# RWKV blocks of a hybrid decoder layer: three bursts laid out on four quadrants, the group norm's passes moved to ScalarE, and the buffers, loads and order that go with it

## The chip, the cores and the metric

The kernel runs on one core of a Trainium2 chip. A core has a matrix engine (TensorE, PE in the rows; its weight loads are a row kind of their own, PEld) and three others that work on tiles: VectorE (DVE), ScalarE (ACT) and GpSimd (POOL). SyncE (SP) issues most DMA transfers. Each engine takes its instructions strictly in the order in which the program lists them and waits, where it must, on semaphores of the others. The metric is the device time of one execution in microseconds (us), the median of several runs.

## The reference

One decoder layer on 2048 tokens of width 1024. An adaLN-modulated RMS norm feeds one input projection. Half of its columns go to an RWKV-7 group (8 heads of 64), half to a stick-breaking attention group. Both are gated, projected out together and added back. The change lies in the RWKV group:

```python
def step(state, inp):
    r_t, w_t, k_t, v_t, kk_t, b_t = inp
    sa = jnp.einsum('bhij,bhj->bhi', state, -kk_t)
    state = (state * w_t[:, :, None, :]
             + sa[..., None] * b_t[:, :, None, :]
             + v_t[..., None] * k_t[:, :, None, :])
    y_t = jnp.einsum('bhij,bhj->bhi', state, r_t)
    return state, y_t
...
mean = jnp.mean(y, axis=-1, keepdims=True)
var = jnp.mean(jnp.square(y - mean), axis=-1, keepdims=True)
y = (y - mean) * lax.rsqrt(var + GN_EPS)
y = y * ln_w.reshape(H, N) + ln_b.reshape(H, N)
y = y + jnp.sum(rf * kf * r_k, axis=-1, keepdims=True) * vf
return y * jax.nn.silu(g)
```

The kernel doesn't step token by token. It takes chunks of 64 tokens; inside a chunk the recurrence becomes a triangular 64x64 system, which is inverted, and only one state per chunk is carried on.

## The kernel before

The first part of the program (norm, projections of the attention group, attention; up to about 1036 us) is left as it is. From about 1044 us the RWKV group runs in 16 blocks. Block n is one pair of heads (j = 0 to 3) and 512 tokens (b = 0 to 3, eight chunks); b = 0 begins a new pair. A block's work is written as stages, and the loop of step n interleaves three streams by weights: `stage_c(n)`; `stage_gtl(n)`, which runs the group norm of block n-1 (`stage_g`), then `stage_t`, `stage_l` and `stage_z` of block n+1; and `stage_pw(n+2)` with `stage_p` (projections, keys, the chunk matrices and their inversion). Each `yield` hands over to another stream, and its number is the cost that the interleaving books. A scheduler then turns the listing into one fixed order for each engine.

What each stage does, by tile names and lines:
- `stage_p`: 72 matmuls `pss` of 128x512 a block (L370 to L372) project r, k and v; ACT (L399) and DVE (L400 to L403) shift them by a token. `stage_x` makes the chunk matrices with two bursts `x` (L974), each with four masking operations on DVE (L979) that write `mn` and `mt`. Then `mn` goes out (`dn`, L986, SP) and comes back in rows as `pb` (L988). `invert` solves the 16x16 diagonal pieces on DVE (L789 to L816), writes them out (`dt`, L992) and loads them as `t16` (L997), whose second half `t16[:, 1]` is the inverse's diagonal.
- `stage_t`: transposes into `tmp`, `vp`, `ap`, then burst `bvp` (L1033); ACT copies the results (L1013, L1021, L1027, L1036).
- `stage_l`: burst `fp` (L1047) takes `mn` and `t16`; DVE masks it (`ft`, L1051); three bursts `xp` with additions (`rf`) finish the inverse.
- `stage_z`: burst `zp` (L1080), copied by ACT into `at` (L1084) and `zg` (L1088); bursts `mr` (L1096), `np` (L1110) and `y0` (L1113); DVE makes `mtt` and `rq` (L1101, L1103), `n0` (L1116).
- `stage_c`: eight chunk steps, each a matmul `sp` (L1134) and a DVE operation `sall` (L1135), then burst `yr` (L1144) and the sum `ysb` (L1148).
- `stage_g`: statistics of `ysb` on DVE (L1163, L1164), `vr` (L1166), the power -1/2 on POOL (L1167), two passes over `ysb` on POOL (L1169, L1170), the transposes `ytp` (L1174), and the additions and the gate.

`burst()` holds a list of small matmuls together as one unbroken row on TensorE. `z_ps`, `mm_ps`, `tr_ps` and `av_ps` hand out PSUM tiles; `z_ps` has two buffers, which `x`, `zp`, `np`, `y0`, `fp` and `xp` share, so a burst waits until the copies of the tile two before it are done. Matrices of 64x64 use a quarter of the array (a quadrant: 64 rows by 64 columns); `HS[e]` is one half of the partitions. In the bursts `mr` and `yr` all four quadrants are used; in `fp`, `bvp` and `zp` an operand's half and the result's half are the same or tied, so that two quadrants are.

Of the kernel before, what the change touches and what calls it, by code (L numbers as in the profile page):

```python
# [18 lines left out]
P = 128  # L19
# [69 lines left out]
def trunk(nc, a, out):  # L89
# [10 lines left out]
    words = 23848  # L100
# [40 lines left out]
    crow = cp.tile([8, P], F32, name="crow")  # L141
# [12 lines left out]
    rows = cp.tile([P, P], F32, name="rows")  # L154
# [208 lines left out]
    pace = [None]  # L363

    def inproj(w, b, name):
        wh, wl = w[0], w[1]
        ps = mm_ps(name)
        for k in range(KB):
            with tc.issue_after(pace[0]) if pace[0] is not None else nullcontext():
                PE.matmul(ps, wh[:, k], hth[b][:, k], start=k == 0, stop=False)  # L370
            PE.matmul(ps, wh[:, k], htl[b][:, k], start=False, stop=False)  # L371
            PE.matmul(ps, wl[:, k], hth[b][:, k], start=False, stop=k == KB - 1)  # L372
            yield 0.65
        return ps
# [445 lines left out]
    @contextmanager  # L820
    def burst():
# [7 lines left out]
        mms = behind + [i for i in traced[start:] if i.engine == first[0].engine]  # L829
        behind[:] = mms[-1:]  # L830
# [21 lines left out]
    def stage_p(n):  # L852
# [9 lines left out]
        else:  # L862
            lz = [rp_.tile([P, TB], F32R, tag=t, name="lz" + t) for t in ("lw", "th")]
# [94 lines left out]
    def stage_x(n):  # L958
# [43 lines left out]
    def stage_t(n):  # L1002
# [24 lines left out]
        A.activation(out=ab[:, :, :, 0, :].rearrange("p i h d -> p (i h) d"),  # L1027
                     in_=ap.rearrange("p (c d) -> p c d", c=8), func=AF.Copy)
        bvp = z_ps("bvp").rearrange("p (c d) -> p c d", c=8)
        with burst():  # L1030
            for i, h in IH:
                for e in (1, 0):
                    PE.matmul(bvp[HS[e], 2 * i + h], mn[i // 2][HS[1 - e], e, i % 2, h], zg[HS[1 - e], e, i, h],  # L1033
                              start=True, stop=True)
        yield 0.9
        A.activation(out=ab[:, :, :, 1, :].rearrange("p i h d -> p (i h) d"), in_=bvp, func=AF.Copy)  # L1036

    def stage_l(n):
# [32 lines left out]
    def stage_z(n):  # L1071
# [4 lines left out]
        zp = [z_ps("zp").rearrange("p (c m d) -> p c m d", c=4, m=2) for _ in range(2)]  # L1076
# [74 lines left out]
    def stage_g(n):  # L1151
# [28 lines left out]
    def stage_pw(n):  # L1180
# [4 lines left out]
        yield from stage_p(n)  # L1185
        if j < 3:
            if b > 0:
                yield from w_split(("rk", "rr", "rv")[b - 1], j + 1)
            if b < 3:
                w_load(("rk", "rr", "rv")[b], j + 1)  # L1190

    def stage_gtl(n):
# [6 lines left out]
        if n + 1 < NST:  # L1199
            yield from stage_l(n + 1)  # L1200
# [9 lines left out]
    _merge((stage_gtl(-1), 13.5), (stage_pw(1), 22))  # L1210
# [81 lines left out]
    for n in range(NST):  # L1292
        jobs = [(_prio(tc, stage_c(n), 100), 13), (stage_gtl(n), 17.5)]
# [42 lines left out]
```

## Time and profile before

| | |
|---|---|
| median of 3 runs | 1912.5 us (1912.26 to 1915.36) |
| the profiled execution | 1910.53 us, its span 1908.8 us |
| mean granted TensorE clock | 0.971 of full speed |
| busy: PE, DVE, ACT, POOL | 90%, 71%, 46%, 40% of the span |
| RWKV blocks, start of `fp` to start of the next | 37.1 to 46.0 us, 15 intervals from 1101.5 to 1722 us, 41.4 us on average |

The profiled execution lies 2.0 us below the median. A row of a timeline gives the start, the duration, the engine, the line and operation, the tiles (output<-inputs) with their shapes, a count of like instructions in succession, and in brackets the idle time of the engine before it and what ended that. Matmuls overlap, so the duration of a row of many is best read from the starts of the rows.

### The profile page before, as it was taken

What the parts mean: (1) busy time and instruction counts of PE and PEld (TensorE: products, weight loads), DVE (VectorE), ACT (ScalarE), POOL (GpSimd) and SP (SyncE); (2) the same over time, 40 slices, a digit from 0 to 9 for tenths busy, and PEclk for the clock granted to TensorE, in tenths of its full rate; (3) what the DMA queues carried; (4) which work ended last, traced back from release to release, by engine and by line L of the source; (5) the groups of instructions that cost most, each with busy time, mean ns of one, the idle gap of its engine ahead of it and who ended that gap; (6) DMA issues with size and microseconds to landing.
All of it is one profiled execution on the core that took longest, in us unless ns stands there. A gap on an engine that the chain in (4) does not pass through costs nothing. (4 is left out here: it accounts for less than half of the span.)

```text
span 1908.8 us, 38922 instructions
## 1 busy us (share of the span) xinstructions
PE 1719.8 (90%) x14880; PEld 1161.5 (61%) x14880; DVE 1348.7 (71%) x2855; ACT 870.0 (46%) x1718; POOL 754.6 (40%) x1106
## 2 busy tenths in 40 slices
PE   7979889999899998999997898898899888989998
PEld 2646556666566665667654455665555565667886
DVE  4876788577776778768775667877877777775542
ACT  2665567366654656546654333323332333422221
POOL 1425466355643646445444223222223232223322
PEclk9889999999999999999998899999999999999999
DMA  8442201222123221132111423222333333236442
GB/s 298 150 116 56 56 26 50 64 64 70 37 56 81 67 56 42 51 92 67 45 50 56 133 55 83 68 60 74 77 81 81 80 77 107 75 94 179 149 138 89
DMA packets 210408, 159.93 MB, mean 84 GB/s; under 512 B 113247, under 2 KB 171820, under 8 KB 210222
## 3 DMA queue, kind: packets, MB, share of 16 engines
q1 hardware_dynamic: 209220, 155.31, 29.2%
q8 instruction: 117, 1.92, 0.4%
q10 hardware_dynamic: 1002, 2.13, 0.4%
q14 instruction: 69, 0.57, 0.1%
HBM read 94.48 MB, written 44.04 MB: 73 GB/s over the span
## 5 line engine op out<-in xcount | busy, mean ns | idle before, releaser
L523 POOL TENSOR_TENSOR s<-s,u 128x512 f32<-128x512 f32 (+2 forms) x320 | 305.8, 963 | 216.5 <-ACT s L511 102.0
L540 DVE TENSOR_TENSOR al<-tr,ah 128x512 fp32r<-128x512 f32 (+1 forms) x320 | 187.4, 599 | 96.3 <-ACT ah L539 95.7
L522 DVE TENSOR_TENSOR_SCAN u<-u,dmask 128x512 f32<-128x512 f32 x192 | 240.0, 1268 | 13.0 <-ACT u L510 11.4
L539 ACT ACTIVATE ah<-tr 128x512 fp32r<-128x512 f32 (+1 forms) x320 | 171.7, 553 | 103.7 <-PE tr L535 99.6
L510 ACT ACTIVATE u<-z 128x512 f32<-128x512 f32 (+2 forms) x320 | 173.4, 555 | 73.4 <-PE z L507 49.0
L535 PE MATMUL tr<-kept_ident,s 128*128 128x128 f32 x1088 | 173.5, 279 | 33.1 <-DVE al L540 26.5
L511 ACT ACTIVATE s<-z 128x512 f32<-128x512 f32 (+2 forms) x320 | 166.2, 549 | 53.0 <-PE tr L535 53.0
L535 PEld LDWEIGHTS tr<-kept_ident,s 128*128 128x128 f32 x1088 | 130.3, 143 | 74.9 <-DVE al L540 38.4
L370 PE MATMUL pss<-kept_hh,kept_wh 128*128 128x512 f16 x416 | 161.3, 388 | 8.8 <-PEq L730 8.8
L372 PE MATMUL pss<-kept_hh,kept_wl 128*128 128x512 f16 x416 | 160.9, 387 | 0.0
L371 PE MATMUL pss<-kept_hl,kept_wh 128*128 128x512 f16 x416 | 160.9, 387 | 0.0
L372 PEld LDWEIGHTS <-kept_wl 128*128 128x128 f16 x928 | 93.2, 100 | 104.9 <-issue 14.2
L370 PEld LDWEIGHTS <-kept_wh 128*128 128x128 f16 x928 | 94.3, 102 | 101.4 <-issue 29.2
L371 PEld LDWEIGHTS <-kept_wh 128*128 128x128 f16 x928 | 93.0, 100 | 94.8 <-issue 25.0
L506 PE MATMUL z<-kt,qt 128*128 128x512 f32 (+2 forms) x320 | 132.1, 417 | 9.5 <-issue 3.7
L553 PE MATMUL av<-ah,vt 128*128 128x512 f32 (+1 forms) x320 | 136.5, 427 | 3.9 <-DVE o L564 2.3
L554 PE MATMUL av<-al,vt 128*128 128x512 f32 (+1 forms) x320 | 136.0, 426 | 0.2 <-DVE al L540 0.2
L507 PE MATMUL z<-kt,qt 128*128 128x512 f32 (+2 forms) x320 | 117.5, 371 | 0.0
L519 DVE TENSOR_TENSOR_SCAN u<-u,dmask 128x128 f32<-128x128 f32 (+3 forms) x128 | 107.3, 867 | 11.6 <-ACT u L510 6.6
L370 PE MATMUL psg<-kept_hh,kept_wh 128*128 128x512 f16 x256 | 99.1, 387 | 10.9 <-DVE klo L434 4.8
L1274 PE MATMUL po<-kept_woh,kept_yh 128*128 128x512 f32 x256 | 102.3, 400 | 0.0
L1275 PE MATMUL po<-kept_wol,kept_yh 128*128 128x512 f32 x256 | 101.5, 397 | 0.0
(296 smaller groups left out, 4146.1 us busy)
## 6 DMA issues: line engine op xcount, KB each, us to landing
kept_raw<-in_w_in SPq DMA_DIRECT2D x29, 512.0 KB, 4.3
ad<-in_ada_w SPq DMA_DIRECT2D x24, 512.0 KB, 5.6
qt<-qt SPq DMA_DIRECT2D x48, 256.0 KB, 3.3
xt<-in_x SPq DMA_DIRECT2D x16, 512.0 KB, 5.1
y<-sg SPq DMA_DIRECT2D x32, 256.0 KB, 2.3
t<-dt SPq DMA_DIRECT2D x64, 128.0 KB, 3.2
xr<-in_x SPq DMA_DIRECT2D x16, 512.0 KB, 3.6
out<-xr SPq DMA_DIRECT2D x16, 512.0 KB, 2.6
```

What stands on the lines that cost most here:

```text
L370: PE.matmul(ps, wh[:, k], hth[b][:, k], start=k == 0, stop=False)
L371: PE.matmul(ps, wh[:, k], htl[b][:, k], start=False, stop=False)
L372: PE.matmul(ps, wl[:, k], hth[b][:, k], start=False, stop=k == KB - 1)
L510: A.activation(out=u[:, 0:nk], in_=z[:, 0:nk], func=AF.Sigmoid, scale=-0.125)
L511: A.activation(out=s[:, 0:nk], in_=z[:, 0:nk], func=AF.Sigmoid, scale=0.125)
L522: V.tensor_tensor_scan(out=ur, data0=ur, data1=mr, initial=u[:, nk:nk + 1], op0=ALU.mult, op1=ALU.bypass)
L523: G.tensor_tensor(out=s[:, 0:nk], in0=s[:, 0:nk], in1=u[:, 1:nk + 1], op=ALU.mult)
L535: PE.transpose(tp[:, q * P:(q + 1) * P], att[gi, q][:, ks * P:(ks + 1) * P], ident)
L539: A.activation(out=ah[:, r], in_=tp[:, r], func=AF.Copy)
L540: V.tensor_tensor(out=al[:, r], in0=tp[:, r], in1=ah[:, r].bitcast(F32), op=ALU.subtract)
L553: PE.matmul(av[:, r], vs, ah[:, r], start=first, stop=False, skip_group_check=True)
L554: ins = PE.matmul(av[:, r], vs, al[:, r], start=False, stop=last, skip_group_check=True)
```

## The change

Three bursts are laid out anew. In `fp`, `bvp` and `zp` the half of the output is now `e ^ h` or depends on it, so that each burst goes over all four quadrants. `fp` and `bvp` each fill half of two PSUM tiles (one of `z_ps`, one of `mm_ps`), so that the operations that read them are two in place of one. Each of the two `zp` tiles is now filled by matmuls of the whole burst; `at` is copied by four operations of 64x256 in place of two of 128x256, `zg` by four of 64x256 as before. The copy of `ap` becomes four operations. `t16[:, 1]` changes its halves by parity, and its load becomes four DMAs in place of two.

The group norm's two passes on POOL go; a small DVE operation `nm` makes -mean times `vr`, and eight ACT operations of 128x64 (one per head and 128 tokens) apply `vr` as scale and `nm` as bias.

The rest: `fp`'s burst is tied behind the latest projection matmul that has been listed (`burst(True)`); five more `yield`s stand ahead of `stage_l`, and two stream weights change; `lz` (the low-rank columns) has two buffers of its own in place of those of `lw` and `th`; `invert` takes its scratch from `at`'s buffer; the load of the next pair's weights stands after the ninth `yield` of the next block's `stage_p` in place of at the end of a block; two small tiles of the first part move to another pool.

```diff
-        fp = z_ps("fp").rearrange("p (c d) -> p c d", c=8)
-        with burst():
+        fp = [f("fp").rearrange("p (i d) -> p i d", i=8) for f in (z_ps, mm_ps)]
+        with burst(True):
             for i, h in IH:
                 for e in (1, 0):
-                    PE.matmul(fp[HS[e], 2 * i + h], mn[i // 2][HS[e], e, i % 2, h], t16[HS[e], 0, 2 * i + h],
+                    PE.matmul(fp[e][HS[e ^ h], i], mn[i // 2][HS[e], e, i % 2, h], t16[HS[e], 0, 2 * i + h],
                               start=True, stop=True)
-        V.tensor_tensor(out=ft, in0=fp, in1=_bc(fmask, [P, 8, 64]), op=ALU.mult)
+        for e in range(2):
+            V.tensor_tensor(out=ft[:, e::2], in0=fp[e][:, 0:4], in1=_bc(fmask, [P, 4, 64]), op=ALU.mult)
...
-                    PE.matmul(zp[i // 2][HS[e], 2 * (i % 2) + h].rearrange("p m d -> p (m d)"), rf[HS[e], 2 * i + h],
-                              ab[HS[e], i, h].rearrange("p m d -> p (m d)"), start=True, stop=True)
-        yield 1.8
-        for g in range(2):
-            A.activation(out=at[:, 2 * g:2 * g + 2].rearrange("p i h d -> p (i h) d"), in_=zp[g][:, :, 0, :],
-                         func=AF.Copy)
+                    f = e ^ h
+                    PE.matmul(zp[f][HS[e], i].rearrange("p m d -> p (m d)"), rf[HS[f], 2 * i + e],
+                              ab[HS[f], i, e].rearrange("p m d -> p (m d)"), start=True, stop=True)
+        yield 0.9
+        for e in range(2):
+            for h in range(2):
+                A.activation(out=at[HS[e], :, h, :], in_=zp[e ^ h][HS[e], :, 0, :], func=AF.Copy)
...
-        G.tensor_tensor(out=y8, in0=y8, in1=_bc(mv[:, :, 0:1], [P, 8, 64]), op=ALU.subtract)
-        G.tensor_tensor(out=y8, in0=y8, in1=_bc(vr, [P, 8, 64]), op=ALU.mult)
+        nm = sm.tile([P, 8, 1], F32, name="nm")
+        V.scalar_tensor_tensor(out=nm, in0=mv[:, :, 0:1], scalar=-1.0, in1=vr, op0=ALU.mult, op1=ALU.mult)
+        for q in range(8):
+            yq = ysb[:, q // 2, q % 2]
+            A.activation(out=yq, in_=yq, func=AF.Identity, scale=vr[:, q], bias=nm[:, q])
...
         if n + 1 < NST:
+            for _ in range(5):
+                yield 0.6
             yield from stage_l(n + 1)
...
-    _merge((stage_gtl(-1), 13.5), (stage_pw(1), 22))
+    _merge((stage_gtl(-1), 14.5), (stage_pw(1), 22))
...
-        jobs = [(_prio(tc, stage_c(n), 100), 13), (stage_gtl(n), 17.5)]
+        jobs = [(_prio(tc, stage_c(n), 100), 13), (stage_gtl(n), 18.2)]
```

The fixed order of the engines changes with it. The block shown is the one whose `fp` starts at 1228.25 us in the profile of before. On ScalarE, around its `stage_z` (`t` is a projection of v on its way, `y` the copy of `y0`), before:

```order
L399 ACTIVATE t_20255<-pss,kept_um_19416 128x512
L331 ACTIVATE kept_wl_314<-kept_ident_61,m_20489 128x128
L1084 ACTIVATE at<-zp 128x256
L1088 ACTIVATE zg<-zp 64x256 x2
L1084 ACTIVATE at<-zp 128x256
L1088 ACTIVATE zg<-zp 64x256 x2
L1118 ACTIVATE y_20493<-y_20437 128x512
L399 ACTIVATE t_20473<-pss,kept_um_19965 128x512
```

and now, with the lines of the new program:

```order
L332 ACTIVATE kept_wl_317<-kept_ident_61,m_20702 128x128
L400 ACTIVATE t_20319<-pss,kept_um_19446 128x512
L1188 ACTIVATE ysb<-ysb,nm,vr 128x64
L1102 ACTIVATE at<-zp 64x4x64 x4
L1105 ACTIVATE zg<-zp 64x4x64 x4
L400 ACTIVATE t_20545<-pss,kept_um_20014 128x512
L1188 ACTIVATE ysb<-ysb,nm,vr 128x64 x7
L1134 ACTIVATE y_20543<-y_20460 128x512
```

One of the eight group-norm operations now stands ahead of the copies of `zp`, and the projection `t` of v directly behind them. This is the order in 11 of the 16 blocks; in three of the four with b = 0 the copies stand first, and the first block has no group norm at that place.

On VectorE, from `vr` of the group norm over the masks of the second burst `x` to the operations on `mr`, before:

```order
L1166 TENSOR_SCALAR vr<-mv 128x8
L979 TENSOR_TENSOR mn<-x_20338,kept_xmask_240 128x4x64
L979 TENSOR_TENSOR mt<-x_20338,kept_xmask_240 128x2x2x64
L979 TENSOR_TENSOR mn<-x_20339,kept_xmask_240 128x4x64
L979 TENSOR_TENSOR mt<-x_20339,kept_xmask_240 128x2x2x64
L1101 TENSOR_TENSOR mtt<-mr,kept_id_70 64x4x64 x2
```

and now:

```order
L1182 TENSOR_SCALAR vr<-mv 128x8
L1185 SCALAR_TENSOR_TENSOR nm<-mv,vr 128x8
L401 COPY t_20704<-nxt 128x1
L403 COPY nxt<-t_20545 128x1
L404 SCALAR_TENSOR_TENSOR vt<-pss,kept_u_20015,t_20545 128x512
L985 TENSOR_TENSOR mn<-x_20402,kept_xmask_243 128x4x64
L985 TENSOR_TENSOR mt<-x_20402,kept_xmask_243 128x2x2x64
L985 TENSOR_TENSOR mn<-x_20403,kept_xmask_243 128x4x64
L985 TENSOR_TENSOR mt<-x_20403,kept_xmask_243 128x2x2x64
L1117 TENSOR_TENSOR mtt<-mr,kept_id_70 64x4x64 x2
```

The operation `nm` and the one on v (`vt`, which reads ACT's `t`) have come between `vr` and the masks. This is so in six blocks.

On TensorE, from the last matmul of the first burst `x` to the start of the second, before:

```order
L974 MATMUL x_20288<-ar,bk 64x128
L1080 MATMUL zp<-ab,rf 64x128 x16
L370 LDWEIGHTS kept_wh_287
L370 MATMUL pss<-kept_hh_384,kept_wh_287 128x512
L974 MATMUL x_20338<-ar,bk 64x128
```

and now:

```order
L980 MATMUL x_20352<-ar,bk 64x128
L1097 MATMUL zp<-ab,rf 64x128
L371 LDWEIGHTS kept_wh_290
L371 MATMUL pss<-kept_hh_387,kept_wh_290 128x512
L372 LDWEIGHTS kept_wh_290
L372 MATMUL pss<-kept_hl_388,kept_wh_290 128x512
L373 LDWEIGHTS kept_wl_291
L373 MATMUL pss<-kept_hh_387,kept_wl_291 128x512
L371 LDWEIGHTS kept_wh_290
L371 MATMUL pss<-kept_hh_387,kept_wh_290 128x512
L1097 MATMUL zp<-ab,rf 64x128 x15
L372 LDWEIGHTS kept_wh_290
```

The burst `zp` is parted after its first matmul by four matmuls `pss`, and the last row shown begins eight more that stand ahead of the second `x`; before there was one. (The program lists the 16 matmuls of a burst `zp`; the trace has each twice, x32.)

## Rows read from the trace of the kernel before

**Rows 1.** Windows: stretch, its length, busy time of PE, PEld, DVE, ACT, POOL, clock.

```profile
1200.00:1300.00 100.00, 91.87 (x1261) 61.27 (x1261) 78.30 (x240) 34.63 (x63) 28.69 (x25) 1.00 0.30 71
```

**Rows 2.** Waits of TensorE, 1150 to 1690 us (13 blocks): total, times, longest.

```profile
PE sp L1134 <- DVE sall L1135: 15.7, 20, 1.7
PE zp L1080 <- DVE mt L979: 11.4, 10, 1.2
PE pn L924 <- ACT sq L916: 8.2, 8, 3.4
PE y L1113 <- DVE mt L979: 4.5, 3, 1.5
```

**Rows 3.** Timeline of TensorE in one block, and `fp` of a later one.

```profile
1228.25 1.15 PE L1047 MATMUL fp<-t,mn 64*64 64x64 f32 x32
1229.34 0.39 PE L372 MATMUL pss<-kept_hh,kept_wl 128*128 128x512 f16 x1
1229.56 0.38 PE L370 MATMUL pss<-kept_hh,kept_wh 128*128 128x512 f16 x1
...
1234.79 0.69 PE L1144 MATMUL yr<-sall,rq 64*64 64x64 f32 x32
1235.30 1.06 PE L974 MATMUL x<-ar,bk 64*64 64x128 f32 x32
1236.19 1.04 PE L1080 MATMUL zp<-ab,rf 64*64 64x128 f32 x16
1238.46 1.09 PE L1080 MATMUL zp<-ab,rf 64*64 64x128 f32 x16 [1.23 <-DVE mt L979]
...
1266.64 1.15 PE L1047 MATMUL fp<-t,mn 64*64 64x64 f32 x32
...
1353.26 1.15 PE L1047 MATMUL fp<-t,mn 64*64 64x64 f32 x32
```

**Rows 4.** Timeline of ScalarE in the same block: copies of `zp`, and `t` of v.

```profile
1239.59 0.38 ACT L1084 ACTIVATE at<-zp 128x256 f32<-128x256 f32 x1 [1.27 <-PE zp L1080]
1239.87 0.76 ACT L1088 ACTIVATE zg<-zp 64x256 f32<-64x256 f32 x2
...
1246.96 0.69 ACT L399 ACTIVATE t<-pss,kept_um 128x512 f32<-128x512 f32 x1 [2.52 <-PE pss L372]
```

**Rows 5.** Timeline of GpSimd in the same block: the group norm.

```profile
1240.66 1.64 POOL L1167 TENSOR_TENSOR vr<-vr,kept_mhalf 128x8 f32<-128x8 f32 x1
1242.38 1.04 POOL L1170 TENSOR_TENSOR ysb<-ysb,vr 128x512 f32<-128x512 f32 x1
```

**Rows 6.** Timeline of VectorE in the same block, and the inversion's last step of the later one.

```profile
1239.55 0.17 DVE L1166 TENSOR_SCALAR vr<-mv 128x8 f32<-128x8 f32 x1
...
1241.96 0.41 DVE L979 TENSOR_TENSOR mt<-x,kept_xmask 128x256 f32<-128x256 f32 x1
...
1248.02 0.17 DVE L794 COPY pr<-pb 64x8 f32<-64x8 f32 x1 [0.61 <-DMA pb<-dn]
...
1248.31 0.74 DVE L403 SCALAR_TENSOR_TENSOR vt<-pss,kept_u,t 128x512 f32<-128x512 f32 x1
...
1256.58 0.37 DVE L816 COPY pr<-pr 64x256 f32<-64x256 f32 x1
...
1341.57 0.37 DVE L816 COPY pr<-pr 64x256 f32<-64x256 f32 x1
```

**Rows 7.** Timeline of SyncE's issues in the same block, and the page's row of them.

```profile
1259.12 3.10 SPq L997 DMA_DIRECT2D t<-dt  x4
t<-dt SPq DMA_DIRECT2D x64, 128.0 KB, 3.2
```

**Rows 8.** The tile `fp`: idle time of its engine until this load, and times.

```profile
  DMA t<-dt: 2.6, 1
```

**Rows 9.** Timeline of TensorE after its longest wait.

```profile
1305.97 1.14 PE L924 MATMUL pn<-kept_hm,sq 128*128 128x2 f32 x8 [3.40 <-ACT sq L916]
1307.35 0.63 PE L370 MATMUL pss<-kept_hh,kept_wh 128*128 128x512 f16 x1
```

More of the change, by code (lines that the diff above doesn't have):

```diff
@@ L139, in trunk @@
     V.tensor_copy(out=id2[64:128], in_=ident[64:128, 64:128])
-    crow = cp.tile([8, P], F32, name="crow")
+    sbk = stage.enter_context(ExitStack())
+    kp = sbk.enter_context(tc.tile_pool(name="kv", bufs=1))
+    xctx = ExitStack()
+    rowp = xctx.enter_context(tc.tile_pool(name="rows", bufs=1))
+    crow = rowp.tile([8, P], F32, name="crow")
     DMA.dma_start(out=crow, in_=a["c"][0].rearrange("(r c) -> r c", c=P))
@@ L153, in trunk @@
     V.tensor_tensor(out=cact, in0=cact, in1=cps[:, 0:8], op=ALU.mult)
-    rows = cp.tile([P, P], F32, name="rows")
+    rows = rowp.tile([P, P], F32, name="rows")
     col = {}
@@ L371, in inproj @@
             PE.matmul(ps, wh[:, k], htl[b][:, k], start=False, stop=False)
-            PE.matmul(ps, wl[:, k], hth[b][:, k], start=False, stop=k == KB - 1)
+            latest[0] = PE.matmul(ps, wl[:, k], hth[b][:, k], start=False, stop=k == KB - 1).ins
             yield 0.65
@@ L820, in burst @@
     @contextmanager
-    def burst():
+    def burst(proj=False):
         traced = tc.nc.cur_bb.bb.instructions
@@ L829, in burst @@
         mms = behind + [i for i in traced[start:] if i.engine == first[0].engine]
+        if proj:
+            new = next(i for i in mms if i not in behind)
+            tc.add_manual_dep(new, latest[0].name, mybir.DependencyInfo(mybir.DependencyClass.NoSync,
+                                                                        mybir.DependencyReason.DATA), reason="burst")
         behind[:] = mms[-1:]
@@ L862, in stage_p @@
         else:
-            lz = [rp_.tile([P, TB], F32R, tag=t, name="lz" + t) for t in ("lw", "th")]
+            lz = [rp_.tile([P, TB], F32R, tag=f"lz{m}", name="lz") for m in range(2)]
             for m in range(2):
@@ L995, in stage_x @@
         for e in range(2):
-            for m in range(2):
-                DMA.dma_start(out=t16[HS[e], m], in_=dt[m, e].rearrange("c s t -> s c t")[0:64])
+            DMA.dma_start(out=t16[HS[e], 0], in_=dt[0, e].rearrange("c s t -> s c t")[0:64])
+        for e in range(2):
+            for f in range(2):
+                DMA.dma_start(out=t16[HS[f], 1].rearrange("p (i x) t -> p i x t", x=2)[:, :, e],
+                              in_=dt[1, e].rearrange("(i h) s t -> h s i t", h=2)[e ^ f, 0:64])
     IH = [(i, h) for i in range(4) for h in range(2)]
@@ L1026, in stage_t @@
         yield 0.44
-        A.activation(out=ab[:, :, :, 0, :].rearrange("p i h d -> p (i h) d"),
-                     in_=ap.rearrange("p (c d) -> p c d", c=8), func=AF.Copy)
-        bvp = z_ps("bvp").rearrange("p (c d) -> p c d", c=8)
+        apv = ap.rearrange("p (i h d) -> p i h d", i=4, h=2)
+        for h in range(2):
+            for e in range(2):
+                A.activation(out=ab[HS[e ^ h], :, e, 0, :], in_=apv[HS[e], :, h, :], func=AF.Copy)
+        bvp = [f("bvp").rearrange("p (i d) -> p i d", i=8) for f in (z_ps, mm_ps)]
         with burst():
@@ L1032, in stage_t @@
                 for e in (1, 0):
-                    PE.matmul(bvp[HS[e], 2 * i + h], mn[i // 2][HS[1 - e], e, i % 2, h], zg[HS[1 - e], e, i, h],
+                    PE.matmul(bvp[e][HS[e ^ h], i], mn[i // 2][HS[1 - e], e, i % 2, h], zg[HS[1 - e], e, i, h],
                               start=True, stop=True)
-        yield 0.9
-        A.activation(out=ab[:, :, :, 1, :].rearrange("p i h d -> p (i h) d"), in_=bvp, func=AF.Copy)
+        yield 0.5
+        for e in range(2):
+            A.activation(out=ab[:, :, e, 1, :], in_=bvp[e][:, 0:4], func=AF.Copy)
     def stage_l(n):
@@ L1075, in stage_z @@
         at = rw.tile([P, 4, 2, 64], F32, tag="at", name="at")
-        zp = [z_ps("zp").rearrange("p (c m d) -> p c m d", c=4, m=2) for _ in range(2)]
+        zp = [z_ps("zp").rearrange("p (i m d) -> p i m d", i=4, m=2) for _ in range(2)]
         with burst():
@@ L1184, in stage_pw @@
             rw_start(j)
[L1185 to L1190, printed above, removed]
+        for i, c in enumerate(stage_p(n)):
+            yield c
+            if i == 8 and j < 3 and b > 0:
+                w_load(("rk", "rr", "rv")[b - 1], j + 1)
+        if j < 3 and b > 0:
+            yield from w_split(("rk", "rr", "rv")[b - 1], j + 1)
     def stage_gtl(n):
```

22 lines of the change are left out of this document (10 added, 12 removed).

## The prediction, as it was put on record

> **What bounds the kernel now.** I read the windows first. In the RWKV stretch TensorE is busy 92% of the time and VectorE 78%, while ScalarE and GpSimd stand near a third [rows 1]; the clock is at its full 2.4 GHz level there. TensorE is therefore the first account: what it is spared counts unless it turns into a wait. The waits of TensorE come next. The four largest groups of 13 blocks, 15.7, 11.4, 8.2 and 4.5 us [rows 2], are 39.8 us, or 3.1 us a block; most blocks could not gain more by removing waits alone. The timeline of one block comes third: `fp` starts at 1228.25 and at 1266.64 us, a period of 38.4 us, and TensorE's row is nearly closed [rows 3].
>
> A second account runs beside it, since the rows of a block depend on each other from one to the next. I follow it in the same block, from the start of `zp` at 1236.19 [rows 3]. The second burst `x` gives the masks, and the last one ends at 1241.96 + 0.41 = 1242.37, 6.2 us after the start. Through two DMA steps (out to `dn` and back as `pb`) the inversion starts at 1248.02, 5.65 us later, and its last copy at 1256.58, after 8.56 us [rows 6]. The four loads of `t16` are issued from 1259.12 over 3.1 us, and one lands 3.2 us after its issue [rows 7]: the last issue is near 1261.5, the landing near 1264.7, 8.1 us after the copy. `fp` starts 1.9 us behind that [rows 3], and 7.94 us lie between `fp` and its `zp` (1228.25 to 1236.19). 6.2 + 5.65 + 8.56 + 8.1 + 1.9 + 7.94 is again 38.4. So this loop over `zp`, masks, inversion, `fp` has a reserve of only 1.9 us; in the later block of the rows the copy is at 1341.57 and `fp` at 1353.26, 11.7 us, a reserve of 3.6 [rows 3, 6]. In one block it was used up: `fp` waited 2.6 us for the load [rows 8].
>
> **The change part by part.** *Bursts.* `fp` takes 1.09 us from its start to the next row's; `yr`, as many matmuls of the same shape in four quadrants, takes 0.51 (1234.79 to 1235.30). That spares 0.58, and as much for `bvp`, which has the same shape and count. `zp` takes two halves of 1.04 and 1.09 by their durations, 2.04 by the pitch of about 1.02 each; `x`, as many matmuls of its shape in four quadrants, takes 0.89 (1235.30 to 1236.19) [rows 3]. That spares 1.1. Together 2.26 us a block, or 36 us in 16. All of it is TensorE time in a stretch where TensorE is busy, so all of it counts in the first account.
>
> *Copies.* A copy of 256 columns takes 0.38 us on ScalarE for 128 partitions and 0.76 / 2 for 64 [rows 4]: halving the partitions saves nothing. `at` and `zg` go from six copies (2.3 us) to eight (3.0 us). The halves of the `ap` copy go from one operation to four of the 256-column kind, 4 x 0.38 = 1.5 us. With ScalarE busy a third, this time itself is covered; what counts is who waits for the last copy. Before, the copies of the first half ran while the second half was still waiting; now every `zp` tile needs the whole burst, and so all copies come after it.
> The Trainium skill says in "TensorEngine Tiling (Array Packing)", Performance Considerations, PSUM Bottleneck, that tiling makes TensorE faster but not the evacuation of PSUM, which may then be the limit. The trace agrees, with a burst of 0.9 us and copies of 3.0. By this rule alone `zp`'s share, 1.1 x 16 = 18 of the 36 us, would be lost; the forecast below takes the loss from the order of the copies instead.
>
> *Group norm.* Two passes of 1.04 us each (one stands in the rows) leave GpSimd [rows 5], which TensorE did not wait for. Eight operations of 128x64 go to ScalarE: between 0.2 and 0.38 us each (no row shows the shape; the 256-column copies bound it above, and below I halve them), 0.3 taken, 2.4 us a block. The cost is in the order. In 11 blocks the first of the eight stands ahead of `at`. It needs `nm`, that needs the power on GpSimd, and that needs `vr`, which starts only at 1239.55, 3.36 us after `zp` [rows 6]. From `zp`'s start: `vr` done at 3.5, power 1.64 [rows 5] to 5.2, `nm` 0.17 to 5.4, one operation to 5.7. Only then can `at` be copied, at 3.4 us before (1239.59 [rows 4]). Four copies end at 7.2, three of `zg` at 8.35. The second `x` needs the PSUM tile that this seventh copy frees. TensorE reaches it with a first `zp` matmul, the wait for the masks of the first `x` until 2.27 (1238.46 [rows 3]; the four `pss` between lie inside it), the other 15 until 3.2 and eight `pss` at 0.22 (1229.34 to 1229.56 [rows 3]) at 4.9. The **new wait is 3.4 us**, in 11 blocks 37 us: what the bursts spared. Only waits further on in a block (`sp`, `pn`, `y`) could shrink for it.
>
> *The loop.* In six of those blocks the masks of the second `x` also stand behind `vt`, which needs ScalarE's `t` of v behind the eight copies: copies to 8.7, `t` 0.69 [rows 4] to 9.4, `vt` 0.74 [rows 6] to 10.2, four masks at 0.35 to 11.6. That is 5.4 later than 6.2. In the other five the masks follow `x` (8.35 + 0.9) at 10.7, 4.5 later. The rest of the loop is as it was: 5.65 + 8.56 + 8.1, and 7.94 less 0.58. The loads of `t16` are six, but the pair that `fp` needs is still within the first six issues of SyncE, where the old four and the two `dt` were; I take no difference, and 0.8 us (one issue of 3.1 / 4 [rows 7]) as an end. So the block of the rows goes from 38.4 to 11.6 + 5.65 + 8.56 + 8.1 + 7.36 = 41.3, **2.9 us longer**. Its TensorE account would give 38.4 - 2.26 + 3.4 = 39.5; the longer one decides.
>
> *Sum.* Six blocks at 2.9 are 17. Two blocks, the second and third of the first pair, have `mr` ahead of the second `x`, waiting for `at`; I take 3 each, 6. Three blocks have the masks at 10.7 and longer periods before; between 1.1 (TensorE account) and 2.0 (loop), 1.5 each, 4.5. In three blocks with b = 0 the copies stand first: the bursts' 2.26 less one for the eight copies, -1 each, -3. The first block and the last one's tail have no such wait, -2 each, -4. Together +20.5 on 1910.5, and 2.0 for the distance to the median: **1933 us**.
>
> *The rest.* Own buffers for `lz` let it load earlier (nobody waits for it in the rows): nothing, and 1 us gain at most. The five `yields` and the pin of `fp` move `pss` ahead of `fp`; if `fp` is late anyhow, this costs nothing. The weight load moves out of the way of `dt` on SyncE: 0 to 0.8 us gain in nine blocks. The two halves of `ft` (2 x 0.41 in place of 0.69, from the masks' duration) cost 0.1 a block.
>
> **The rivals.** *Faster, the wait is absorbed (24 in 100).* If the inversion and the loads shorten or the reserve is nearer to 3.6 than 1.9 in most blocks, the loop stays covered; the new wait of 3.4 then takes the place of the waits for `sall`, `sq` and `y`'s masks, 15.7 + 8.2 + 4.5 = 28.4 in 13 blocks, 2.2 a block [rows 2]. A block then gains 2.26 + 2.2 - 3.4 = 1.06, 17 us: 1895. Everything spared and no wait at all would be 1912.5 - 36 = 1876. It decides whether `t16` lands before TensorE arrives at `fp`. Against it: 1.9 us of reserve where 5.4 is asked for.
>
> *No change that can be told (8 in 100).* TensorE's account alone balances: 37 us of waits against 36, with a part absorbed: 1909 to 1916. (A measurement of this kernel tells 0.2%, 3.8 us, from none.)
>
> *Slower still, by the clock (8 in 100).* After the longest wait of TensorE, 3.40 us, six `pss` in a row took 0.63 us in place of 0.38 (the first stands in the rows [rows 3, 9]): the lower level of 1.2 GHz. If each of 11 waits of that length brings six at 0.25 more, 1.5 us, this adds 16.5: 1950. For it: the length is the same. Against: one such spell is all I see, and near it TensorE had shorter waits as well.
>
> *The bursts don't shorten (2 in 100)*, because halves of one tile hinder each other: 1933 + 36 at most where TensorE decides, about 1955 with the loop deciding in half of the blocks. `yr` and `x` speak against it.
>
> **How the numbers follow.** The forecast, slower through the loop, has 58 in 100, with a range of its own of 1916 to 1949: the reserve at 3.6 in place of 1.9 in all 11 blocks takes 17 off, the 0.8 at the loads and longer group-norm operations (0.08 x 8) in 11 blocks add 16. With the faster case included and the two slowest cases cut at the edge, the range is 1890 to 1952. Chances: faster 0.24, same 0.08, slower 0.68.
>
> **What would show it.** Right, if the profile of the changed kernel has TensorE waiting some 3 us at the second `x` in most blocks, put down to ScalarE's `zg`; if `fp` waits for the load of `t16` in six blocks or more, and the plain block's period is 41 us. The bursts are right if `fp` takes 0.5 and `zp` 0.9 from start to start; the wait's cause, if the first 128x64 operation ends 5.7 us after `zp`. Wrong, if `vr` comes much earlier than 3.4 us after `zp`, if `fp` starts without a wait, or if the waits at `sp` go.

## The result, and the profile after

| | before | after |
|---|---|---|
| median of 4 runs each | 1912.38 us (1912.15 to 1915.36) | 1966.54 us (1965.37 to 1968.87) |
| profiled execution, its span | 1910.53, 1908.8 us | 1965.89, 1964.0 us |
| mean granted TensorE clock | 0.971 | 0.953 |

The change makes the kernel slower: the medians lie 54 us apart, and the ratio on record is 1.0265, with an interval of 1.0240 to 1.0291 (46 to 56 us). The direction was forecast, the size was not: +20.5 was expected, and the time lies beyond the range.

The windows come first. The columns are stretch, length, busy time of PE, PEld, DVE, ACT and POOL (with counts), granted clock, share and rate of the DMAs. The RWKV part from 1040 us to the end, of before:

```profile
1040.00:1908.80 868.80, 780.87 (x8954) 536.05 (x8954) 581.16 (x1647) 270.54 (x499) 249.08 (x228) 0.98 0.35 95
```

and of after:

```profile
1040.00:1964.00 924.00, 791.21 (x8954) 533.01 (x8954) 586.63 (x1681) 337.90 (x723) 213.24 (x196) 0.93 0.33 89
```

TensorE executes the same 8954 matmuls. It is idle for 132.8 us in place of 87.9, and it is busy for 10 us more although three bursts became shorter. The clock, 0.93 in place of 0.98, is why. To part the two, I took all TensorE rows of this stretch, from the start of each to the start of the next. The first row is the first projection of the RWKV part, at 1044.89 us before and 1046.45 after. Idle time (from 0.15 us on) is "waits"; half of the busy time at the granted clock of 0.5 (the 1.2 GHz level) is "clock"; the rest is "work", as it would be at 2.4 GHz. The half is an estimate: the slow `mr` shown below loses 0.77 of its 1.75 us.

| RWKV part to the end | waits | clock | work |
|---|---|---|---|
| before | 71.8 | 15.5 | 767.2 |
| after | 116.0 | 49.3 | 742.7 |
| difference | +44.2 | +33.8 | -24.5 |

The sum, +53.5, is the longer stretch but for 1.7 us, and 1.6 of these lie ahead of the first row. So the bursts did spare TensorE some 25 us, new waits took 44, and the slower clock took 34 beside them. The 1.2 GHz level held for 34 us in 7 stretches before, for 118 us in 22 stretches after (those that begin behind the first row).

The waits of TensorE after (1150 to 1690 us, total, times, longest), the counterpart of [rows 2]:

```profile
PE x L980 <- ACT zg L1105: 22.5, 7, 3.9
PE sp L1150 <- DVE sall L1151: 15.0, 14, 1.6
PE pn L930 <- ACT sq L922: 12.1, 11, 2.5
PE fp L1062 <- DMA t<-dt: 10.3, 5, 3.6
PE zp L1097 <- DVE mt L985: 8.3, 9, 0.9
PE mr L1112 <- ACT at L1102: 5.8, 2, 3.4
```

The first, fourth and last line are new. `sp` is hardly smaller than in [rows 2], `zp` is smaller by a quarter, and `pn` is larger by half. A plain block on TensorE, as [rows 3] shows it of before:

```profile
1240.47 0.81 PE L1062 MATMUL fp<-t,mn 64*64 64x64 f32 x32 [1.71 <-DMA t<-dt]
1241.21 0.65 PE L944 MATMUL n<-kept_ident,nr 128*128 128x128 f32 x4
...
1247.45 1.05 PE L980 MATMUL x<-ar,bk 64*64 64x128 f32 x32
1248.34 0.38 PE L1097 MATMUL zp<-ab,rf 64*64 64x128 f32 x2
1248.65 0.39 PE L371 MATMUL pss<-kept_hh,kept_wh 128*128 128x512 f16 x1
...
1250.60 1.10 PE L1097 MATMUL zp<-ab,rf 64*64 64x128 f32 x30 [0.92 <-DVE mt L985]
1251.63 0.39 PE L372 MATMUL pss<-kept_hl,kept_wh 128*128 128x512 f16 x1
...
1253.15 0.38 PE L373 MATMUL pss<-kept_hh,kept_wl 128*128 128x512 f16 x1
1256.55 1.10 PE L980 MATMUL x<-ar,bk 64*64 64x128 f32 x32 [3.02 <-ACT zg L1105]
1257.48 1.05 PE L1112 MATMUL mr<-mt,at 64*64 64x128 f32 x32
1258.46 1.15 PE L1126 MATMUL np<-zg,mt 128*64 128x64 f32 x32
```

Its releasers on GpSimd, ScalarE and VectorE (compare [rows 4 to 6]):

```profile
1251.95 1.64 POOL L1183 TENSOR_TENSOR vr<-vr,kept_mhalf 128x8 f32<-128x8 f32 x1 [7.17 <-DVE vr L1182]
```

```profile
1253.82 0.44 ACT L1188 ACTIVATE ysb<-ysb,nm,vr 128x64 f32<-128x64 f32 x1 [13.86 <-DVE nm L1185]
1254.16 1.29 ACT L1102 ACTIVATE at<-zp 64x256 f32<-64x256 f32 x4
1255.47 1.31 ACT L1105 ACTIVATE zg<-zp 64x256 f32<-64x256 f32 x4
1256.80 0.69 ACT L400 ACTIVATE t<-pss,kept_um 128x512 f32<-128x512 f32 x1
1257.38 2.42 ACT L1188 ACTIVATE ysb<-ysb,nm,vr 128x64 f32<-128x64 f32 x7
```

```profile
1257.52 0.15 DVE L403 COPY nxt<-t 128x1 f32<-128x1 f32 x1 [3.67 <-ACT t L400]
1257.59 0.74 DVE L404 SCALAR_TENSOR_TENSOR vt<-pss,kept_u,t 128x512 f32<-128x512 f32 x1
1258.25 0.42 DVE L985 TENSOR_TENSOR mn<-x,kept_xmask 128x256 f32<-128x256 f32 x1
...
1259.24 0.42 DVE L985 TENSOR_TENSOR mt<-x,kept_xmask 128x256 f32<-128x256 f32 x1
...
1265.93 0.17 DVE L795 COPY pr<-pb 64x8 f32<-64x8 f32 x1 [2.05 <-DMA pb<-dn]
...
1273.61 0.37 DVE L817 COPY pr<-pr 64x256 f32<-64x256 f32 x1
```

The reader can follow the forecast wait link by link. ScalarE idles until `nm`, 2 us after the end of `zp`. One group-norm operation runs, then `at`, then `zg`; TensorE stands 3.02 us at the second `x`. VectorE idles 3.67 us at v's column copy, with the masks behind it in its queue. (The group-norm operation stands ahead of the copies in 11 blocks; `t` of v stands directly behind them in six of these.)

The clock is best seen in a later block, whose second `x` waited 2.80 us:

```profile
1342.32 1.10 PE L980 MATMUL x<-ar,bk 64*64 64x128 f32 x32 [2.80 <-ACT zg L1105]
1343.24 1.82 PE L1112 MATMUL mr<-mt,at 64*64 64x128 f32 x32
1344.99 1.95 PE L1126 MATMUL np<-zg,mt 128*64 128x64 f32 x32
```

and in the windows over the wait and behind it:

```profile
1339.00:1343.40 4.40, 1.60 (x43) 1.10 (x45) 0.17 (x1) 3.75 (x12) 0.35 (x1) 1.00 0.10 15
1343.40:1346.80 3.40, 3.40 (x70) 3.07 (x60) 3.06 (x9) 1.59 (x5) 0.00 (x0) 0.50 0.22 36
```

The clock is granted in full over the wait and falls to 0.50 just after it; `mr` takes 1.75 us from its start to the next row's, where it takes 0.98 in the plain block (1257.48 to 1258.46). Ten of the 22 stretches stand at or behind a wait at the second `x` (eight) or at `mr` (two); the others follow waits at `pn` (five), `fp`, `sp` and a few more. It is not so each time: of nine waits at the second `x`, 2.80 to 3.89 us long, the plain block's 3.02 is the one that no slow stretch follows (granted clock 1.00 from 1256.50 to 1262.00).

### The profile page after: what moved, and what is told of

Same layout as the page of the kernel before. It is cut to its first block, busy times and chain, and to the rows that moved or that the text cites. A ratio compares the mean times of both kernels' runs of the same rounds, so it can differ in the third digit from the quotient of the medians.

```text
span 1964.0 us, 39059 instructions
## 1 busy us (share of the span) xinstructions
PE 1727.5 (88%) x14880; PEld 1155.3 (59%) x14880; DVE 1352.0 (69%) x2887; ACT 937.3 (48%) x1942; POOL 719.5 (37%) x1074
## 5 line engine op out<-in xcount | busy, mean ns | idle before, releaser
L523 DVE TENSOR_TENSOR_SCAN u<-u,dmask 128x512 f32<-128x512 f32 x192 | 240.0, 1268 | 12.7 <-ACT u L511 11.4
L511 ACT ACTIVATE u<-z 128x512 f32<-128x512 f32 (+2 forms) x320 | 173.6, 556 | 72.5 <-PE z L508 49.3
L536 PE MATMUL tr<-kept_ident,s 128*128 128x128 f32 x1088 | 173.3, 279 | 33.9 <-DVE al L541 27.2
L507 PE MATMUL z<-kt,qt 128*128 128x512 f32 (+2 forms) x320 | 131.7, 416 | 10.1 <-ACT s L512 4.1
L1188 ACT ACTIVATE ysb<-ysb,nm,vr 128x64 f32<-128x64 f32 x128 | 45.3, 428 | 148.9 <-DVE nm L1185 148.8
L520 DVE TENSOR_TENSOR_SCAN u<-u,dmask 128x128 f32<-128x128 f32 (+3 forms) x128 | 107.3, 867 | 11.6 <-ACT u L511 6.4
L936 POOL TENSOR_TENSOR ar<-kn,ep 128x512 f32<-128x512 f32 x15 | 23.3, 1556 | 229.0 <-ACT kn L920 229.0
```

The source lines that it names most:

```text
L511: A.activation(out=u[:, 0:nk], in_=z[:, 0:nk], func=AF.Sigmoid, scale=-0.125)
L523: V.tensor_tensor_scan(out=ur, data0=ur, data1=mr, initial=u[:, nk:nk + 1], op0=ALU.mult, op1=ALU.bypass)
L536: PE.transpose(tp[:, q * P:(q + 1) * P], att[gi, q][:, ks * P:(ks + 1) * P], ident)
```

## The experiments

Theory A: the new wait at the second `x` comes from the order on ScalarE, and the clock loss from the waits. Theory B: the loop `zp`, masks, inversion, `fp` has no reserve, so that it costs time in each block whatever TensorE does. Rival C: the four-quadrant bursts themselves are at fault (more copies of a PSUM tile that is free later, or a lower clock by themselves). Rival D: the group norm on ScalarE costs time by its 2.75 us a block alone.

The account of each run, as above (first projection of the RWKV part to the end; ratio to the runs of before on the same chip):

| run | ratio, interval | waits | clock | work |
|---|---|---|---|---|
| before | 1 | 71.8 | 15.5 | 767.2 |
| after | 1.0265 (1.0240, 1.0291) | 116.0 | 49.3 | 742.7 |
| e1_gn_pool | 1.0075 (1.0060, 1.0090) | 98.6 | 26.6 | 744.6 |
| e2_before_gn_act | 1.0032 (1.0014, 1.0050) | 78.6 | 20.3 | 766.8 |
| e3_ysb_behind | 1.0075 (1.0045, 1.0105) | 99.0 | 26.3 | 745.1 |
| e4_masks_first | 1.0029 (1.0004, 1.0054) | 92.2 | 24.1 | 744.2 |
| e5_by_tile | 1.0061 (1.0039, 1.0083) | 92.2 | 26.8 | 748.8 |
| e6_no_pace | 1.0234 (1.0179, 1.0290) | 118.9 | 43.3 | 742.7 |
| e7_wait_filled | one run, 1961.96 us | 94.3 | 33.6 | 779.8 |
| e8_before_wait | one run, 2004.71 us | 137.8 | 50.5 | 762.6 |
| e12_bursts_alone | 1.0243 (1.0213, 1.0274) | 118.4 | 39.6 | 742.6 |
| e13_before_short | 0.9931 (0.9905, 0.9958) | 66.3 | 17.9 | 762.6 |
| e14_e4_short | 0.9835 (0.9799, 0.9871) | 67.1 | 13.6 | 747.6 |

### Group norm: its work, or its place in the queue?

e1_gn_pool is the changed kernel with the two passes back on GpSimd:

```diff
-        for q in range(8):
-            A.activation(out=yq, in_=yq, func=AF.Identity, scale=vr[:, q], bias=nm[:, q])
+        G.tensor_tensor(out=y8, in0=y8, in1=_bc(mv[:, :, 0:1], [P, 8, 64]), op=ALU.subtract)
+        G.tensor_tensor(out=y8, in0=y8, in1=_bc(vr, [P, 8, 64]), op=ALU.mult)
```

> The changed kernel with the group norm's two passes back on GpSimd; everything else of the change stays. Theory (the first group-norm operation ahead of `at` holds TensorE at the second `x`, and each such wait is followed by a stretch at the lower clock level): the wait x<-zg falls from 25.3 us in all to under 10, the time at half clock behind 1040 us falls from 118 us to under 60, and the time comes to 1905 to 1925. Rival (the eight copies of the new layout hold the loop, wherever the group norm runs): the wait stays near 3 us a block and the time stays above 1950.

e2_before_gn_act is the kernel before with the opposite edit alone.

> The kernel before with only the group norm's passes on ScalarE. In its order all eight operations stand behind the copies of `zp`. Theory: nothing waits for them, 1905 to 1916, no x<-zg wait. Rival (ScalarE operations of 128x64 with scale and bias are dear in themselves, or the later `ysb` delays `ytp`): 1925 or more.

e3_ysb_behind is the changed kernel with only the order altered: each of the eight operations is tied behind the last copy of `zg` on ScalarE.

```diff
+            tc.add_manual_dep(g1, zlast[0].name, mybir.DependencyInfo(mybir.DependencyClass.NoSync, ...))
```

> The changed kernel with one thing altered: the eight group-norm operations are tied behind the last copy of `zp` on ScalarE. Theory: the copies start at 3.4 instead of 5.7 us after `zp`, the wait at the second `x` falls from 3.4 to about 1 us a block, and with it the half-clock stretches that follow; 1900 to 1925, within 5 us of the kernel with the group norm on GpSimd. Rival (loop through masks, inversion and `fp`): `vt` still stands ahead of the masks in six blocks, so fp<-t16 stays at 10 us and the time above 1940.

Measured: 1930.25, 1920.39 and 1930.28 us. In the same block of e3, ScalarE now copies first, and the eight operations still run there:

```profile
1247.91 1.31 ACT L1102 ACTIVATE at<-zp 64x256 f32<-64x256 f32 x4 [12.63 <-PE zp L1097]
1249.23 1.31 ACT L1105 ACTIVATE zg<-zp 64x256 f32<-64x256 f32 x4
1250.56 0.69 ACT L400 ACTIVATE t<-pss,kept_um 128x512 f32<-128x512 f32 x1
1251.15 2.75 ACT L1189 ACTIVATE ysb<-ysb,nm,vr 128x64 f32<-128x64 f32 x8
```

and the wait at `x` is a fraction of what it was (1150 to 1690 us):

```profile
PE sp L1151 <- DVE sall L1152: 22.3, 23, 2.0
PE fp L1062 <- DMA t<-dt: 12.4, 4, 4.4
PE pn L930 <- ACT sq L922: 10.5, 11, 1.9
PE zp L1097 <- DVE mt L985: 9.2, 10, 0.9
PE x L980 <- ACT zg L1105: 5.9, 8, 1.5
```

One changed order gives back 36 us, as much as taking the whole group norm off ScalarE (e1); that is the wait's cause. Both runs lie 5 us above their forecast of up to 1925. D is small: where the operations stand behind the copies, their 2.75 us a block make no difference between e3 and e1. It isn't shown to be nothing: e2 lies 0.3% above before, between its two forecasts, and its masks end about 0.6 us later after `zp` (6.8 against 6.2 in three of the plain blocks); what that costs is not shown. In the account e3 has 17.0 us of waits and 23.0 of clock less than after. The wait at `x` went from 22.5 to 5.9 us, but waits at `sp` and `fp` took half of that back, and none of the stretches at 1.2 GHz (67 us, 11 of them) stands behind the second `x` any more.

### Does a wait bring the clock down, or does the burst?

e7_wait_filled is the changed kernel with 20 or 21 extra matmuls in eight blocks, put where TensorE would wait; their result is overwritten.

```diff
+        if n in {3: 21, 5: 21, ...}:
+            with burst():
+                for _ in range({3: 21, 5: 21, ...}[n]):
+                    PE.matmul(mr0[0], W["rk", (n + 1) // 4][0][:, 0], hth[(n + 1) % 4][:, 0], start=True, stop=True)
```

> The changed kernel with 21 matmuls of 128x512 (20 in two blocks), whose result is overwritten, between `zp` and the second `x` in eight of the blocks that wait there; they belong to no result. The copies come no earlier, TensorE only works through the time. Theory (the clock falls because TensorE stood idle): no stretch at half clock begins within 6 us behind the second `x` in these eight blocks, where seven of eight had one. Rival (the clock falls for another reason, such as the burst that follows): the stretches stay. The time is no test here: the extra matmuls take 4.5 us a block where the wait was 3 to 3.9, and they move eight `pss`.

e8_before_wait makes such a wait in the kernel before, whose bursts are the old ones: nine extra copies on ScalarE ahead of `at`, overwritten by it.

```diff
+        for _ in range(9):
+            A.activation(out=at.rearrange("p i h d -> p (i h d)"), in_=zp[0].rearrange("p c m d -> p (c m d)"), func=AF.Copy)
```

> The kernel before with nine more copies of the first `zp` tile into `at` ahead of the real ones, so that ScalarE is late by about 5 us and TensorE waits at the second `x` or at `mr`; the bursts and the group norm are as before. Theory: where the wait is 3 us or more, a stretch at half clock follows within 6 us in most blocks, and the time behind 1040 us at half clock goes from 34 us to over 80; the time goes above 1960. Rival (the half-clock stretches belong to the four-quadrant bursts): they stay at 34 to 50 us, and the time grows by the waits alone.

The block of e7 that answers to the one above, with its window:

```profile
1331.23 4.71 PE L1104 MATMUL mr<-kept_hh,kept_wh 128*128 128x512 f16 x21
1336.17 1.10 PE L980 MATMUL x<-ar,bk 64*64 64x128 f32 x32 [0.23 <-ACT zg L1111]
1337.10 1.05 PE L1117 MATMUL mr<-mt,at 64*64 64x128 f32 x32
```

```profile
1336.00:1340.40 4.40, 4.23 (x131) 3.99 (x132) 3.01 (x9) 3.01 (x10) 0.00 (x0) 1.00 0.12 19
```

The copies come no earlier, but TensorE works in the meantime, and the clock stays at 1.00; no stretch at 1.2 GHz is left behind the second `x` of those eight blocks, and the clock loss falls by 15.7 us. A ninth block, left unfilled, keeps its wait of 3.89 us and its slow stretch. The RWKV part gets no shorter (917.2 us against 917.5, one run), because the extra work, 37.1 us, is as much as the waits and the clock loss give up together, 21.7 and 15.7. In e8 the old bursts at a provoked wait show the reverse:

```profile
1451.28 1.98 PE L974 MATMUL x<-ar,bk 64*64 64x128 f32 x32 [4.49 <-ACT zg L1090]
1453.04 1.93 PE L1098 MATMUL mr<-mt,at 64*64 64x128 f32 x32
```

```profile
1449.00:1456.00 7.00, 4.72 (x86) 4.40 (x88) 2.35 (x7) 2.90 (x8) 0.26 (x1) 0.51 0.04 9
```

+66.0 us of waits brought +35.0 of clock loss. So the clock follows the waits, with either kind of burst; that part of C falls. The loss was 0.4 to 0.8 of the added waits: 33.8 to 44.2 (after), 35.0 to 66.0 (e8), 24.1 to 46.6 (e12), 10.8 to 27.2 (e3), 4.8 to 6.8 (e2). The Trainium skill says in "TensorE: Matmul & The Clock Gate", Loop structure matters more than you think, that the loop nest decides whether TensorE keeps its clock: matmuls back to back keep it, a long wait for a DMA between all of them loses it. The traces agree that waits lose it; here single waits for ScalarE did (2.80 us, granted clock 0.50 behind it).

### The loop

e4_masks_first is e3 with `vt` tied behind the masks of the second `x` on VectorE; e5_by_tile is e4 with the eight copies of `zp` listed by PSUM tile, so that the first tile is free after four.

```diff
+            tc.add_manual_dep(vi, maskl[0].name, ...)      # e4, e5
```

```diff
-        for e in range(2):
-            for h in range(2):
-                A.activation(out=at[HS[e], :, h, :], in_=zp[e ^ h][HS[e], :, 0, :], func=AF.Copy)
+        for f in range(2):
+            for e in range(2):
+                A.activation(out=at[HS[e], :, e ^ f, :], in_=zp[f][HS[e], :, 0, :], func=AF.Copy)
+            for e in range(2):
+                A.activation(out=zg[HS[e], e, :, e ^ f, :], in_=zp[f][HS[e], :, 1, :], func=AF.Copy)
```

> As the run before, and the `vt` operation on VectorE is tied behind the masks of the second `x`. If the loop is what costs, this is faster than the run before by 1 us or more in each of six blocks, 6 to 15 us in all, and fp<-t16 goes to near 0; if the wait at `x` and the clock were all, it is within 4 us of the run before.

> As e4_masks_first, and the eight copies are listed by `zp` tile, so that the tile that the second `x` waits for is free after four copies instead of seven, 1.1 us earlier. Theory: x<-zg (7.4 us in e4) goes to under 2, and the loop gains up to 1 us a block: 1895 to 1912. If the remaining cost is elsewhere (the load of `t16`, `sq`), within 4 us of e4.

e4 measured 1918.08 us, 12 below e3, as forecast: earlier masks seem worth time, though the two intervals overlap. e5, 1924.54, gains nothing more although its wait at `x` is smaller (4.5 us, 7.4 in e4): the copies as such do not bind any longer. Its masks also end 0.8 us earlier after `zp` (7.6 against 8.4) in most blocks; why that gains nothing, no run tells.

e13_before_short and e14_e4_short leave the last doubling step of the inversion out, in the kernel before and in e4; 3.4 us of VectorE's time in each block's loop.

```diff
-        for k in (4, 8):
+        for k in (4,):
```

> The kernel before without the last doubling step of the inversion (four VectorE operations, 3.4 us a block, are left out; what they would fill is not computed). If TensorE binds the kernel before, with its 3.1 us of waits a block, shortening the loop by 3.4 us gives little: 1895 to 1912. If the loop binds it too: 1860 to 1890.

> e4_masks_first without the same step of the inversion (left out as in e13). Theory (the loop takes back what TensorE is spared): fp<-t16 goes from 13.6 us to under 4, and the time falls by 15 to 30, to 1888 to 1903, at least 10 us more than e13 gains on the kernel before. Rival: e4 gains no more than the kernel before does, and something else holds it.

Measured: 1906.43 us, 0.7% below before, and 1886.60, 1.9% below e4 by the ratios (0.9835 to 1.0029). The same cut is worth 13 us in the one and about 37 in the other, and only in e4 are there waits of `fp` that the cut takes away. The tile `fp` of after, idle time of its engine until this load, and times ([rows 8] has 2.6, 1):

```profile
  DMA t<-dt: 20.8, 8
```

of e4 the same row, and then of e14:

```profile
  DMA t<-dt: 23.5, 9
```

```profile
  DMA t<-dt: 1.8, 2
```

That supports B where `fp` waits: in the account e14 has 25.1 us of waits and 10.5 of clock less than e4. It doesn't show B for each block: five plain blocks (the fourth, seventh, eighth, 11th and 12th) keep their period within 1.1 us.

### The bursts, and what paces them

e12_bursts_alone is the kernel before with the three new bursts, their copies and loads, and nothing else of the change. e6_no_pace is e5 without the five `yield`s, the pin of `fp` and the two stream weights.

> The kernel before with the three bursts in four quadrants and what belongs to them (copies, halves of `t16` and its six loads), and nothing else of the change. TensorE's work falls by 25 us. Theory (the loop has no reserve, and the six loads lengthen it): most of that comes back as waits of `fp` for `t16` and half-clock stretches behind them; 1915 to 1955. Rival (TensorE is the bound): 1885 to 1895.

> As e5_by_tile, with the five yields, the pin of `fp` and the two stream weights undone. If the pacing is worth what it costs in order, this is slower than e5 by 4 us or more; if the waits of `fp` for `t16` (13.6 us in e4) and of `pn` for `sq` (12.5) come from it, it is faster by 5 to 15: 1885 to 1900.

Measured: 1956.56 and 1959.29 us, with `fp` waiting for its load (e12, all blocks):

```profile
PE fp L1055 <- DMA t<-dt: 44.9, 11, 8.3
```

So the bursts alone, which spare TensorE 24.6 us, make the kernel 45 us slower, and `fp` comes up for execution before its load is there in 11 of 16 blocks. But that is not the whole cause. The second and third block alone are 15.1 and 14.3 us longer than before: in e12's order 38 and 34 projection matmuls stand there between `fp` and `zp`, 3 and 13 before, and the way from `fp` to `zp` takes 20.9 and 20.6 us in place of 9.3 and 7.9. The five plain blocks are 1.1 us longer on average, although each of their bursts is shorter. The `yield`s, the pin and the weights, which I had costed at nothing, are worth 35 us (e6 against e5); 21 of these fall on the same two blocks, with the same 38 and 34 matmuls. Three runs thus take the +54 apart: everything but the place of the group norm +16 (e1: the bursts, what paces them, the buffers and loads), that place +36 (e3 or e1 against after).

### Attempts at the load of t16

Five runs tried to shorten the loop further, most by bringing the needed half of `t16` earlier. e9_t0_first is e4 with that half's loads issued first; e10_tile_t0 adds e5's copies, e11_tile_t0_pool also the group norm on GpSimd; e15_masks_all is e4 with v's column copies behind the masks too; e16_masks_dt is e15 with the store and loads of the needed half first.

> As e4_masks_first, with the six loads of `t16` in another order on SyncE: the pair that `fp` needs first, the other four behind it (the change has two of the others, and the wait for the second `dt`, ahead of them in most blocks). Theory (the loop's length from the inversion to `fp` now sets the period): the pair lands about 1.6 to 2.9 us earlier after the `dt` issue, fp<-t16 falls from 13.6 to under 7 us, the time by 6 to 15 to 1903 to 1912. Rival (the loop isn't what holds e4): within 4 us of e4, 1914 to 1922.

> As e9, with the copies of `zp` listed by tile as in e5. e5 was no faster than e4 although the second `x` waited less; if the loop takes back what TensorE is spared, this gains with the shorter loop what e5 could not: 1895 to 1910, faster than e9 by 3 or more. If not, within 4 us of e9.

> As e10, with the group norm's passes on GpSimd as before. The group norm alone on ScalarE had cost 0.3% in e2; if that cost is there too, this is 3 to 8 us faster than e10; if GpSimd is in the way of `ar` and `rt`, it is slower.

> As e4_masks_first, and the two one-column copies of v's shift are tied behind the masks too; in e4 they stood ahead of them in about three blocks and waited for ScalarE's `t`, so that the masks ended 11.1 us after `zp` there instead of 8.4. Theory (loop): 3 to 10 us faster than e4, 1908 to 1915. Rival: within 3 us of e4.

> As e15, and on SyncE the store of the half that `fp` needs goes first, its two loads next, then the other four. `fp` could then follow the store by 6.4 us instead of 7.6. Theory (loop): up to 1.2 us in each of the blocks where `fp` waits, 5 to 15 us faster than e15. Rival: within 3 us of e15.

Ratios: 1.0105 (1.0074, 1.0136), 1.0119 (1.0094, 1.0144), 1.0095 (1.0069, 1.0121), 1.0035 (1.0014, 1.0057) and 1.0101 (1.0062, 1.0140). None gained on e4 (1.0029). e11 is 0.2% below e10, as forecast for a small cost of the group norm on ScalarE, but the intervals overlap. In e9 the time from the first store `dt` to `fp` stayed at 7.4 to 8.3 us in the blocks that wait (7.6 to 8.8 in e4). e15 is no test of its theory: in the three blocks with b = 0 meant by it the masks still ended 11.1, 11.1 and 12.7 us after `zp`, as in e4. In e16 the time from the store to `fp` fell to between 6.4 and 7.6 us (7.7 to 9.5 in e15), but the first store came 0.9 us later after the start of the inversion (9.5 against 8.6 on average). Why the order put it there I did not settle.

## Why the prediction was right in direction and wrong in size

*The clock* is the step that failed. I made it a rival, priced by six `pss` at 0.25 us behind each of 11 waits, and gave it 8 in 100, because one spell was all that I saw [rows 9]; the sum has nothing for it. In the account it is 33.8 us. It is no rival of the loop: it comes on top of a forecast that has new waits. Its price in the rival, 16.5 us, was too low as well, since the level lasts over whatever follows (the slow `mr` and `np` above lose 0.8 us each) and since waits at `pn` and `fp` bring it too. It also lengthens the loop itself: in four blocks (the sixth, seventh, tenth and 14th) `fp` starts at the low level, and the way from `fp` to `zp` takes 9.4 to 10.3 us, where I had 7.36 and the plain block has 7.9.

*The sum by blocks.* The period of each block, from `fp` to `fp`, after less before, against the terms of the sum:

| blocks | forecast | measured | clock in it |
|---|---|---|---|
| the five plain ones (`vt` ahead of the masks) | +14.5 | +16.4 | 9.2 |
| second and third | +6 | +17.0 | 7.5 |
| three with the masks behind `x` | +4.5 | +11.7 | 14.9 |
| three with the copies first | -3 | +2.4 | 1.7 |
| first block, last two (one of the six at 2.9), and what lies ahead | -1.1 | +7.7 | 0.5 |

*The second and third block* are the other term that was mis-sized: +9.9 and +7.1 where I took 3 each. Their masks ended 15.2 and 13.1 us after `zp`, 4.9 and 6.3 before and 9.7 in e1: `mr`, ahead of the second `x`, waits there 3.4 and 2.4 us for `at`. I had no account of the loop for these two. For the last row I have none either.

*The plain block* was right link by link: period 41.35 us (1240.47 to 1281.82) against 41.3, and 41.1 and 41.2 in two others. The new wait was 3.02 against 3.4, the masks ended 11.3 us after `zp` against 11.6. The rest of the loop was 6.3 + 8.0 + 7.8 + 7.9 against 5.65 + 8.56 + 8.1 + 7.36: the forecast of `fp` waiting for its load, in six blocks or more, held in eight, in two of them for only 0.3 us.

*Luck* is in the total. Waits and work measured +44.2 - 24.5 = +19.7, next to the forecast of +20.5 without a clock term, but two errors cancel in it: with 36 us spared, +20.5 stood for 56.5 us of new waits. The bursts spare less: over all 16 blocks `fp` went from 17.3 to 10.1 us, `bvp` from 17.3 to 10.3, `zp` from 32.1 to 19.9 (clock and idle time taken out), 26.4 in place of 36. I had read the four-quadrant price from `yr` and `x` [rows 3]; the new bursts reach 0.63 and 1.24 a block, not 0.51 and 0.89. Why, no run tells.

*What I costed at nothing*: the pacing. "If `fp` is late anyhow, this costs nothing" was true of the sum, but without it (e6) the kernel is slower by another 35 us, most of it in two blocks.

*The faster rival* fell as argued: the reserve was used up, and the waits at `sp` did not shrink (15.7 to 15.0). The first account alone, TensorE's busy time, has the wrong sign here: e12 shows 24.6 us less work and 45 us more time.

*The rule on PSUM*, PSUM Bottleneck in the Trainium skill's "TensorEngine Tiling (Array Packing)": the trace agrees that the copies (2.60 us behind a burst of 1.24) become the limit in after, but e3 and e5 show that most of the price was their place in ScalarE's queue and not their duration.

Left open: whether the buffers of `lz`, the scratch in `at`'s buffer or the place of the weights' load cost or gain anything by themselves (not tried), and how e1's 16 us divide. No run here beat the kernel before without leaving work out; e4 is nearest, 0.3% above it.

## What to carry to other kernels

Before a burst is made faster, measure the reserve of the dependence loop that it stands in: with 2 us of reserve, a faster TensorE only waits sooner. Compare the order too: most of what e12 lost lies in two blocks where projections had moved. When work is moved to a less busy engine, look at what it stands in front of in that engine's queue; one operation of 0.44 us ahead of the copies, which itself waited for another engine, cost more than the eight together behind them. And price a new wait of TensorE at more than its length: here each us of added wait brought 0.4 to 0.8 us of loss by the lower clock, by the account's estimate.

## What the runs showed of the hardware

- The clock fell to 1.2 GHz at or behind eight of nine waits of 2.80 to 3.89 us at the second `x`, in an otherwise busy stretch (after); extra matmuls in the gap kept it at 2.4 GHz (e7).
- ScalarE takes 0.33 us for a copy of 64x256 and 0.35 for 128x64 with scale and bias from tiles (2.42 / 7): a quarter of the columns is not cheaper there.
- A burst of 64x64 matmuls became faster by a factor of 1.6 to 1.7, not 2, when it went from two quadrants to four (17.3 to 10.1, 17.3 to 10.3 and 32.1 to 19.9 us in 16 blocks).
